# One instruction per tile in place of two, with the activations pinned, in a split GELU-multiply

The kernel runs on one core of one Trainium2 chip (trn2). The metric is the device time of one execution in microseconds (us), lower is better.

## What is computed

```python
x1, x2 = x[..., :1024], x[..., 1024:]          # x: (32, 512, 2048) float32
out = 0.5 * x1 * (1 + erf(x1 / sqrt(2))) * x2  # (32, 512, 1024) float32
```

So 134.2 MB are read, 67.1 MB are written, and each output element needs one GELU and one multiply.

## The kernel before

The 16,384 rows are cut into 16 tiles of 128 partitions x 8 rows. A tile is loaded whole (64 KB per partition, 8.39 MB) and stored whole (32 KB per partition, 4.19 MB). There are two input and two output buffers, so load i+2 can be issued only when tile i has been consumed.

```python
# cut: the pools, the views of x and out, and the store helper; the whole kernel follows below
def load(i):
    x_tile = xpool.tile([P, R, dim], x.dtype, name="x_tile")   # bufs=2
    nc.sync.dma_start(out=x_tile, in_=x_t[i])
    return x_tile

ahead = [load(0), load(1)]
for i in range(n_tiles):
    x_tile = ahead.pop(0)
    o_tile = opool.tile([P, R, half], out.dtype, name="o_tile")  # bufs=2
    last = i == n_tiles - 1
    for lo, hi in ((0, 1), (1, 2), (2, 4), (4, 8)) if last else ((0, 4), (4, 8)):
        rows = slice(lo, hi)
        nc.scalar.activation(out=x_tile[:, rows, :half], in_=x_tile[:, rows, :half], func=GELU)
        nc.vector.tensor_mul(out=o_tile[:, rows, :], in0=x_tile[:, rows, :half], in1=x_tile[:, rows, half:])
        if last and hi % 4 == 0:
            store(nc.sync, i, o_tile, slice(hi - 4, hi))
    if not last:
        store(nc.sync if i == n_tiles - 2 else nc.scalar, i, o_tile, slice(0, R))
    if i + 2 < n_tiles:
        ahead.append(load(i + 2))
```

The engines named here are ACT (ScalarE), DVE (VectorE) and SP (SyncE, which here only issues transfers). Loads are issued from SP, the stores of tiles 0 to 13 from ACT, the last three stores from SP. ACT thus has two jobs in one instruction stream: GELU, and issuing stores that wait for the multiply on DVE.

## Time and profile before

| | before |
|---|---|
| median of the first 3 executions | 471.6 us (471.53 to 471.65) |
| busy ACT / DVE | 115.4 / 140.5 us (25% / 30%) |
| DMA, moved over the span | 201.35 MB, 428 GB/s |
| spacing of the landings in the middle | 29.0 us |

A landing is the moment at which a transfer is complete. The list of DMA issues has, at the right, the size of one transfer in KB where it is known, and the median time from issue to landing:

```profile
out_dram<-o_tile ACTq DMA_DIRECT2D x14, 4096.0 KB, 41.6
...
x_tile<-in_x_dram SPq DMA_DIRECT2D x16, 45.4
```

The waits of the loading queue are given as total us, times, longest:

```profile
SPq L42 <- DMA x_tile<-in_x_dram: 224.8, 14, 21.2
SPq L42 <- DVE o_tile L58: 174.8, 14, 12.8
```

The second line is the time in which the next load waits for the multiply of the tile that holds its buffer: 174.8 / 14 = 12.5 us per load, which is the time from a landing to the end of that tile's compute.

### The profile page before, as it was taken

To read this page: it belongs to the slowest core of one execution; us is meant where nothing else is said; L and a number is where in the kernel's file an instruction comes from. 1 tells how busy PE (TensorE), PEld (TensorE's weight loads), DVE (VectorE), ACT (ScalarE), POOL (GpSimd) and SP (SyncE) were. 2 spreads that over 40 slices of the span, in tenths; PEclk is the share of its full clock that TensorE was granted. 3 is DMA by queue.
4 is the path that set the end of the run, shared out by engine and by line. 5 is a ranking of instruction groups with operands and counts; after the bars stand their busy time and mean duration, and the time that the engine had idled before them with its cause. 6 is when DMAs were issued, how large, how long until landed. Compare 5 with 4: busy or idle time off the path is not lost.

```text
span 470.1 us, 217 instructions
## 1 busy us (share of the span) xinstructions
DVE 140.5 (30%) x34; ACT 115.4 (25%) x35; POOL 0.2 (0%) x4
## 2 busy tenths in 40 slices
DVE  0070703307043070420705106061150601507042
ACT  1051406024060230603206032060410605105060
POOL 0000000000000000000000000000000000000000
DMA  8999999999999999999999999999999999999988
GB/s 357 446 446 357 443 449 446 402 443 449 402 446 441 435 457 404 432 418 485 407 424 421 488 407 413 432 488 407 402 443 482 413 402 443 472 424 402 480 380 346
DMA packets 4754, 201.35 MB, mean 428 GB/s; under 512 B 528, under 2 KB 528, under 8 KB 528
## 3 DMA queue, kind: packets, MB, share of 16 engines
q1 hardware_dynamic: 2736, 142.61, 70.5%
q10 hardware_dynamic: 2016, 58.72, 28.9%
q14 instruction: 2, 0.02, 0.0%
HBM read 134.22 MB, written 67.11 MB: 428 GB/s over the span
## 4 chain that ended last, share of the span: by engine, by line
DMA 77%; DVE 14%; ACT 7%; issue 0%; ACTq 0%; SPq 0%
DMA x_tile<-in_x_dram 77%; DVE o_tile L58 14%; ACT x_tile L55 7%; ACTq L94 0%; SPq L42 0%; ACTq L55 0%
## 5 line engine op out<-in xcount | busy, mean ns | idle before, releaser
L58 DVE TENSOR_TENSOR o_tile<-x_tile 128x4096 f32<-128x4096 f32 (+2 forms) x34 | 140.5, 4171 | 321.2 <-ACT x_tile L55 321.2
L55 ACT ACTIVATE x_tile<-x_tile 128x4096 f32<-128x4096 f32 (+2 forms) x34 | 114.2, 3407 | 341.0 <-DMA x_tile<-in_x_dram 341.0
L55 ACT ACT_TABLE_LOAD x1 | 1.3, 1283 | 0.7 <-PEq L83 0.7
L83 POOL MEMSET const-bfloat16-1.0<- 128x1 bf16 x1 | 0.1, 102 | 0.0
L83 POOL MEMSET const-uint8-127<- 128x1 uint8 x1 | 0.1, 102 | 0.0
L83 POOL MEMSET const-float32-0.0<- 128x1 f32 x1 | 0.1, 99 | 0.2 <-issue 0.2
L83 POOL MEMSET const-float32-1.0<- 128x1 f32 x1 | 0.1, 99 | 0.0
## 6 DMA issues: line engine op xcount, KB each, us to landing
out_dram<-o_tile ACTq DMA_DIRECT2D x14, 4096.0 KB, 41.6
out_dram<-o_tile SPq DMA_DIRECT2D x1, 4096.0 KB, 24.8
out_dram<-o_tile SPq DMA_DIRECT2D x2, 2048.0 KB, 8.0
x_tile<-in_x_dram SPq DMA_DIRECT2D x16, 45.4
```

The lines of the kernel that those rows point to most:

```text
L55: nc.scalar.activation(out=x_tile[:, rows, :half], in_=x_tile[:, rows, :half], func=GELU)
L58: nc.vector.tensor_mul(out=o_tile[:, rows, :], in0=x_tile[:, rows, :half], in1=x_tile[:, rows, half:],)
L83: nc = _bacc.Bacc("TRN2", target_bir_lowering=False, num_devices=1)
```

## The change

Its intent is fewer, larger instructions in tiles 1 to 14: one activation and one multiply of 8192 elements per partition in place of two of each of 4096. The first tile keeps two halves, the last keeps its four steps. As the compiler's ordering pass may float an early-ready activation ahead of a store on ACT, each activation is pinned behind what the program has put before it on that engine; the pin is an edge of order only, without a wait for data.

```diff
-        for lo, hi in ((0, 1), (1, 2), (2, 4), (4, 8)) if last else ((0, 4), (4, 8)):
+        if last:
+            steps = (0, 1), (1, 2), (2, 4), (4, 8)
+        else:
+            steps = ((0, 4), (4, 8)) if i == 0 else ((0, 8),)
+        for lo, hi in steps:
             rows = slice(lo, hi)
-            nc.scalar.activation(
-                out=x_tile[:, rows, :half], in_=x_tile[:, rows, :half], func=GELU
+            tc.keep_in_program_order(
+                nc.scalar.activation(
+                    out=x_tile[:, rows, :half], in_=x_tile[:, rows, :half], func=GELU
+                )
             )
```

## The prediction

> **What bounds the kernel now.** I read first the page for who is busy, then the chain of work that ended last, then the waits of the loading queue, then the timeline of one tile, and last the packet records of the DMA in the trace. The page's head and its DMA rows:
>
> ```profile
> span 470.1 us, 217 instructions
> DVE 140.5 (30%) x34; ACT 115.4 (25%) x35; POOL 0.2 (0%) x4
> DMA  8999999999999999999999999999999999999988
> DMA packets 4754, 201.35 MB, mean 428 GB/s; under 512 B 528, under 2 KB 528, under 8 KB 528
> ```
>
> The reader is to see that both compute engines idle for over two thirds of the span, while the 16 DMA engines are busy at 90% or more in all but the first and last slices. The table of stretches between landings gives DMA share 1.00 and 434 GB/s from 45 to 335 us, stretch after stretch: the kernel is a steady copy, with the arithmetic beside it. The chain of waits seems to tell another story:
>
> ```profile
> by line: DMA x_tile<-in_x_dram 76.7%; DVE o_tile L58 14.0%; ACT x_tile L55 6.8%; issue 0.3%; ACTq L94 0.2%; SPq L42 0.1%; ACTq L55 0.0%
> ...
> 103.35 3.62 ACT x_tile L55
> 106.98 0.02 issue
> 107.00 8.77 DVE o_tile L58 x2
> 115.78 0.02 issue
> 115.79 45.39 DMA x_tile<-in_x_dram
> 161.18 0.02 issue
> ```
>
> It alternates: half a GELU (3.62), two multiplies (8.77), then a load of 45.39 us that their end lets go, two tiles (58 us) per round. Read literally, the compute is 21% of the path. But 45.39 us is from issue to landing, and most of it is not work: 8.39 MB at 434 GB/s would take 19.3 us alone, and the 12.6 MB that a tile moves in all (8.39 in, 4.19 out) take 29.0 us, exactly the spacing of the landings below. The first part of the 45.39 us is waiting in line behind the load before it. The timeline of tile 2 and of the start of tile 3:
>
> ```profile
> 74.42 7.12 ACT L55 ACTIVATE x_tile<-x_tile 128x4096 f32<-128x4096 f32 x2 [22.10 <-DMA x_tile<-in_x_dram]
> 78.07 8.76 DVE L58 TENSOR_TENSOR o_tile<-x_tile 128x4096 f32<-128x4096 f32 x2 [20.46 <-ACT x_tile L55]
> 86.86 29.27 SPq L42 DMA_DIRECT2D x_tile<-in_x_dram  x2
> 86.86 0.36 ACTq L46 DMA_DIRECT2D out_dram<-o_tile  x1
> 103.35 7.12 ACT L55 ACTIVATE x_tile<-x_tile 128x4096 f32<-128x4096 f32 x2 [21.81 <-DMA x_tile<-in_x_dram]
> ```
>
> Tile 2 lands just before 74.42. Its last multiply ends at 86.83, and at 86.86 load 4 and store 2 are both issued. Tile 3 lands only at 103.3, so load 4 stands 16 us in line before the loading queue is free for it. In the packet records load 4's first packet of 65,536 B starts at 102.82, and store 2's first of 32,768 B at 100.39. Those records also show how the two queues share an engine: one load packet (2.42 us), one store packet (1.21 us), in turn, without a hole, 8 of each per tile on each engine: 8 x 3.63 = 29.0 us. Neither queue is ever empty between the first store (first packet 42.39) and the end of store 13 (about 446). From 446 to the last byte, load 15, store 14 and the two halves of store 15 follow each other in one queue, again without a hole.
>
> **What the Trainium skill says.** (1) "DMA: Bandwidth & Descriptors", section "Queues, rings and completion order": each DMA engine goes round-robin between the queues it has work for and switches at packet boundaries. The trace agrees: load and store packets alternate one for one, as 2.42 and 1.21 us. (2) The same page, "Where 436 GB/s comes from": a fabric ceiling of 435.2 GB/s. The trace's 434 GB/s in the steady stretches is that, within half a per cent: no reordering can be worth much here. (3) "ScalarE: Activation LUTs", "What ACT_TABLE_LOAD costs": an activation with immediate scale and bias takes 186 ns + 0.833 ns per element, and two back to back overlap by about 93 ns. The trace agrees: 1895 ns for 2048 elements (formula 1892), 3601 ns for 4096 (3598), two in 7.12 us. (4) "VectorE: DVE Perf Modes", "The TRN2 errata": fp32 tensor_tensor takes (N+151)/0.96 ns. The trace has 2293 ns at N=2048 (formula 2291) and 4420 at 4096 (4424). The forms in the profile:
>
> ```profile
> L58 DVE TENSOR_TENSOR o_tile<-x_tile 128x4096 f32<-128x4096 f32 x31 | 135.8, 4422 | 304.6 <-ACT x_tile L55 304.6
> L55 ACT ACTIVATE x_tile<-x_tile 128x4096 f32<-128x4096 f32 x31 | 110.4, 3608 | 320.6 <-DMA x_tile<-in_x_dram 320.6
> L55 ACT ACTIVATE x_tile<-x_tile 128x2048 f32<-128x2048 f32 x1 | 1.9, 1895 | 0.0
> ```
>
> **The change, part by part.** Tiles 1 to 14 get one activation and one multiply of 8192 elements instead of two each of 4096; tile 0 and tile 15 keep theirs.
>
> Removed: 14 activations and 14 multiplies. From the durations measured at 2048 and 4096, doubling adds 3601 - 1895 = 1706 and 4420 - 2293 = 2127 ns per 2048 elements, so at 8192: 3601 + 2 x 1706 = 7.01 us for ACT, 4420 + 2 x 2127 = 8.67 us for DVE. Busy time falls by 14 x (2 x 3.60 - 7.01) = 2.7 us on ACT and 14 x (2 x 4.42 - 8.67) = 2.4 us on DVE, to about 112.7 and 138.1 us. Both lie beside the DMA and are worth nothing to the end.
>
> Added: the overlap of GELU with the multiply inside a tile is lost. Before, from landing to the last multiply's end: 3.62 + 0.02 + 8.77 = 12.4 us. After: 7.01 + 0.03 + 8.67 = 15.7 us. So in tiles 1 to 14 the store i and the load i+2 are issued 3.3 us later.
>
> Is that later issue on the path? Three margins answer.
> - Load: 102.82 - 86.86 = 16.0 us between issue and first packet, 12.7 after the change. What a transfer really needs: store 0 was issued at 35.24 into an empty queue on busy engines and its first packet started at 42.39, so 7.15 us (an engine finishes packets already taken). 12.7 is more, and the next load keeps its place.
> - Store: 100.39 - 86.86 = 13.5 us, 10.2 after. Also more than 7.15, by 3 us. So the store queue does not run dry either; this is the narrowest margin.
> - Output buffer: tile i+1's multiply needs store i-1 landed. Store 1 is issued at 57.63 and lands 41.5 us later, 99.2; tile 3's multiply starts at 107.0 before and at 110.4 after. The margin grows from 7.8 to 11.
>
> With no queue ever dry, each packet goes at the moment at which it goes now: landings stay 29.0 us apart, and the 45.4 us from issue to landing shrinks to 42.1 by as much as the compute grew. The end is unchanged too: tile 15 lands at 449.8 as before and keeps its four steps; store 14 is issued at 438.1 instead of 434.8, and its first packet is due at 448.40, 10.3 us on, again above 7.15.
>
> The pinning: an activation of tile i+1 now cannot be ordered ahead of store i on ACT. In the trace of before it was not: the store goes at 86.86 and the next activation starts at 103.35, and the same holds in every other tile. If that order had been the other way, the store would have gone after the landing. So the pins keep what is there, presumably because the longer instruction could have tempted the compiler's ordering. Cost 0; it adds order and no wait on data.
>
> Sum: 0 us on the path that sets the end, of 471.6.
>
> **The rivals.**
> - The chain is right as written and each of its rounds grows by 3.3 us. There are seven full rounds of load, GELU and multiply after the first load, and 7 x 3.3 = 23 us: 495 us, 4.9% slower. For it speaks only the chain; against it the DMA row, which has no hole that a late issue could have caused. I give it 1 to 2%.
> - The store queue misses its turn because the needed lead is more than the 7.15 us seen once. Then the engine takes another load packet in its place; it does not idle. Loads come 1.2 us earlier, stores 2.4 us later, the margin heals by itself, and the backlog of stores is moved after load 15, where the engines are busy anyway. Estimate: 0 to +1 us, 471.6 to 472.6.
> - Faster, through 28 fewer instructions and fewer semaphores: only if the compute were on the path. The most it could be is the fixed costs above, and the DMA's floor of 201.3 MB at 434 GB/s is 464 us, with the start (first packet at 1.74) and the final write's receipt on top. I see at most 1 us.
> - An ordering accident: without knowing the compiler's choice, some load or store could sit behind something on SP or ACT. The pins cover ACT; SP's order follows from the data. One displaced tile would cost at most some 16 us of a hidden wait, so little. 1%.
>
> **Range and chances.** The point is the time of before, 471.6 us. Runs of before spread over 0.12 us; another session could be off by a few tenths; the second rival adds up to 1 us. So the range is 470.8 to 472.8 us. A 2% change is 9.4 us, and only the first and the last rival reach it: slower 0.02, faster 0.01, same 0.97.
>
> **What would show each step.** Right: activations of 8192 elements at 7.0 us and multiplies at 8.7 us, 14 of each; load from issue to landing near 42 us, store near 38 us (41.6 less 3.3); landings still 29.0 us apart; the DMA row unchanged; the last tile starting at 449.9. The chain would show compute at a larger share, near 26%, and the DMA at less, at the same span: that is the proof that the chain's shares were not costs. Wrong: landings more than 29.0 us apart, or a digit under 9 in the middle of the DMA row, which means a queue that ran dry on both sides; or issue to landing still at 45.4 us, which would mean that the first rival is true; or an ACT queue in which a store waits for the next landing.

## The result

The changed kernel took 471.9 us (median of 6 executions, 471.81 to 472.19), the kernel before 471.56 us on the same chip (6 executions, 471.34 to 471.69). The ratio is 1.0008, with a 95% interval of 0.9996 to 1.0021: the same.

The page after, in its head and its DMA rows:

```profile
span 469.8 us, 189 instructions
...
DVE 139.5 (30%) x20; ACT 114.1 (24%) x21; POOL 0.2 (0%) x4
...
DMA  8999999999999999999999999999999999999988
```

There are 28 instructions fewer, 1.3 us less of ACT and 1.0 us less of DVE, and the DMA row is the same digit for digit. The groups by form give the new durations (busy us, mean ns, then the idle time before them):

```profile
L64 DVE TENSOR_TENSOR o_tile<-x_tile 128x8192 f32<-128x8192 f32 x14 | 121.7, 8692 | 281.9 <-ACT x_tile L60 281.9
L60 ACT ACTIVATE x_tile<-x_tile 128x8192 f32<-128x8192 f32 x14 | 98.4, 7029 | 301.7 <-DMA x_tile<-in_x_dram 301.7
```

The chain of work that ended last, to be held against the same stretch of before in the prediction (start, duration, what):

```profile
by line: DMA x_tile<-in_x_dram 71.8%; DVE o_tile L64 13.9%; ACT x_tile L60 11.8%; ACTq L100 0.2%; issue 0.2%; SPq L42 0.1%; ACTq L60 0.0%
...
103.87 7.04 ACT x_tile L60
110.91 0.02 issue
110.93 8.70 DVE o_tile L64
119.64 0.02 issue
119.65 42.14 DMA x_tile<-in_x_dram
161.79 0.02 issue
```

The compute of a round grew from 3.62 + 8.77 to 7.04 + 8.70 us, the load from 119.65 took 42.14 us in place of 45.39, and a round of two tiles ends at 161.79 - 103.79 = 58.00 us after the one before, as it did. What was added at one link was taken off the next one. The waits of the loading queue and the DMA issues say the same in other units:

```profile
SPq L42 <- DVE o_tile L64: 217.9, 14, 15.8
SPq L42 <- DMA x_tile<-in_x_dram: 185.2, 14, 21.0
```

```profile
out_dram<-o_tile ACTq DMA_DIRECT2D x14, 4096.0 KB, 36.9
...
x_tile<-in_x_dram SPq DMA_DIRECT2D x16, 42.1
```

The load's issue waits 43.1 us longer for the multiply in all (217.9 - 174.8) and 39.6 us less for a landing (224.8 - 185.2); issue to landing is 3.3 us shorter. The extra wait for compute was time in which a load would otherwise have stood in line.

### The profile page after: what moved, and what is told of

It is laid out like the page before. It is cut to its first block, busy times and chain, and to the rows that moved or that the text cites. A ratio compares the mean times of both kernels' runs of the same rounds, so it can differ in the third digit from the quotient of the medians.

```text
span 469.8 us, 189 instructions
## 1 busy us (share of the span) xinstructions
DVE 139.5 (30%) x20; ACT 114.1 (24%) x21; POOL 0.2 (0%) x4
## 3 DMA queue, kind: packets, MB, share of 16 engines
q10 hardware_dynamic: 2016, 58.72, 28.9%
## 4 chain that ended last, share of the span: by engine, by line
DMA 72%; DVE 14%; ACT 12%; ACTq 0%; issue 0%; SPq 0%
DMA x_tile<-in_x_dram 72%; DVE o_tile L64 14%; ACT x_tile L60 12%; ACTq L100 0%; SPq L42 0%; ACTq L60 0%
## 5 line engine op out<-in xcount | busy, mean ns | idle before, releaser
L64 DVE TENSOR_TENSOR o_tile<-x_tile 128x8192 f32<-128x8192 f32 (+3 forms) x20 | 139.5, 6985 | 321.6 <-ACT x_tile L60 321.6
L60 ACT ACTIVATE x_tile<-x_tile 128x8192 f32<-128x8192 f32 (+3 forms) x20 | 112.8, 5661 | 341.9 <-DMA x_tile<-in_x_dram 341.9
## 6 DMA issues: line engine op xcount, KB each, us to landing
out_dram<-o_tile ACTq DMA_DIRECT2D x14, 4096.0 KB, 36.9
x_tile<-in_x_dram SPq DMA_DIRECT2D x16, 42.1
```

## The experiments

Twelve kernels were run, and all gave the right result. The theory under test is the prediction's: the time is set by the 16 DMA engines, and a later issue costs nothing so long as the queues still hold work (the full-queue theory). Its first rival is the chain taken literally: every microsecond of compute in a round of two tiles costs one microsecond. "E" in a diff stands for the expression that was there. The listing of the compiled instructions gave the order on each engine before each run.

### The pins alone

```diff
 # kernel before
-            nc.scalar.activation(...)
+            tc.keep_in_program_order(nc.scalar.activation(...))
```

> The kernel before with the pins and nothing else. The listing of its instructions shows the same order on every engine as before, so both theories (the DMA's full queues set the time; the chain's compute sets the time) expect the time of before within 0.1%, about 471.6 us. It also serves as a second profile of the order of before: where the first packet of store 0 falls (42.39 us before, 39.94 us after the change) and the median of store from issue to landing (41.6 before, 36.9 after) tell whether that difference is scatter between executions (then it may move here too) or comes from the whole-tile instructions (then 42.4 and 41.6 again).

Measured: 471.58 us, ratio 1.0003 (0.9988 to 1.0018). Store 0's first packet started at 41.98 us and the store's median from issue to landing was 41.7 us, as before. The pins do nothing to the kernel before, whose order already was that of the program. On the second question the run spoke for the whole-tile instructions, but another run (the last tile whole, below) has the change's instructions up to tile 14 and had 42.31 us and 38.5 us, and a third run with the same first tile (twice and four rows, below) had 39.97: so the 39.94 and 36.9 us of the profile after are scatter between executions, by one packet's turn.

### The whole tiles alone, without pins

```diff
 # kernel after
-            tc.keep_in_program_order(nc.scalar.activation(...))
+            nc.scalar.activation(...)
```

> The change without the pins. The compiler then orders two activations ahead of two stores on ACT in three places (the activations of tiles 5, 9 and 13 stand ahead of the stores of tiles 4, 8 and 12), so those stores wait for the next landing, some 13 to 20 us. Full-queue theory: while the store queue is dry the loads run alone and the engines stay busy; what can be lost is a wait of the multiply of tiles 6, 10 and 14 for an output buffer, 0 to 3 us each, so 471.9 to 481 us. Rival, each displaced store costs its delay: 3 x 13 to 20 us on top, 511 to 532 us.

Measured: 477.99 us, ratio 1.0137 (1.0120 to 1.0154). The timeline shows the first displaced store: tile 4's multiply ends at 147.2, and its store goes only after the GELU of tile 5 has its landing, together with the next one ("16.12 ... x2" spans both):

```profile
138.52 8.69 DVE L62 TENSOR_TENSOR o_tile<-x_tile 128x8192 f32<-128x8192 f32 x1 [20.38 <-ACT x_tile L59]
159.08 7.03 ACT L59 ACTIVATE x_tile<-x_tile 128x8192 f32<-128x8192 f32 x1 [20.59 <-DMA x_tile<-in_x_dram]
159.11 16.12 ACTq L46 DMA_DIRECT2D out_dram<-o_tile  x2
```

That store was 11.9 us late, and three such stores cost 6.4 us in all (477.99 - 471.60), not three times 12. The rival of this run (each delay paid in full) falls. The wait for an output buffer that I had named as the loss did not occur three times but once (16.4 us, at the first multiply of the last tile), and that tile's last multiply still ended 11.8 us after the landing, as it does after the change. The loss lies elsewhere: between 161 and 448 us the rate was 426 GB/s, against 434 from 103 to 161. In the packet records the store queue is empty from 154 to 163, and from about 200 us on load packets last up to 3.3 us where 2.42 is the rule (the median; 1.21 for a packet of half the size). Summed over the run, packets take 5.7 us per engine above their rule, against 1.8 after the change, and the engines end further apart (2.4 us from the first to the last, against 0.9). Why those packets are stretched is not settled by this run. What is shown is that the pins belong to the whole-tile form: without them the change costs 1.4%.

### The first tile whole as well

```diff
 # kernel after
-            steps = ((0, 4), (4, 8)) if i == 0 else ((0, 8),)
+            steps = ((0, 8),)
```

> The first tile whole as well. Load 2 and store 0 are then issued at about 38.4 us instead of 35.1, and the engines take their last packets of load 1 at 38.6 and would be done with them at 41.0. Full-queue theory: here both queues are dry for a moment, for the lead of 4.8 to 7.2 us is not there, so part of the 3.3 us is lost: 1 to 3.3 us, 472.9 to 475.2 us. Rival, issue time is hidden everywhere: 471.9 us.

Measured: 471.46 us, ratio 0.9996 (0.9981 to 1.0011). My expectation failed. Load 2 was issued at 38.49 us and its first packet started at 40.99, 2.5 us later, right behind the last packet of load 1. Since store 0 came later too, load 1 was not slowed by it and landed at 42.0 instead of 45.8. An issue into a queue about to run out thus needs at most 2.5 us here, not the 7.15 us that I had read from store 0: in the packet records of the kernel before, that store, issued at 35.24, stood behind two load packets of each engine (on one they start at 36.1 and 38.6). In this run store 0 still took 5.9 us to its first packet (38.49 to 44.34), behind the first packets of load 2; so the 2.5 us is shown for a load. The halving of the first tile in the changed kernel is worth nothing measurable.

### The last tile whole as well

```diff
 # kernel after
-            steps = (0, 1), (1, 2), (2, 4), (4, 8)
+            steps = ((0, 8),)       # and one store of the whole tile
```

> The last tile whole as well, with one store. Load 15 still lands at 449.4; 7.04 + 8.70 us of compute end at 465.2, and the store of 4 MB needs some 12.5 us (the 2 MB one took 8.0 with 5.0 us of packets, so 3.0 + 9.7): end of the span near 478, 8 us longer, time near 480 us. The engines stand idle from about 458 to 466 us. The chain theory expects about the same here: in the last tile nothing hides the compute. A rise of under 3 us would be against both.

Measured: 478.79 us, ratio 1.0150 (1.0135 to 1.0165), 7.2 us more than before. The stretches of the end show it (us, DVE, ACT, POOL busy, clock, DMA share, GB/s):

```profile
core 0: us, DVE busy (x) ACT busy (x) POOL busy (x), PEclk, DMA share, GB/s
449.00:458.00 9.00, 1.57 (x1) 7.03 (x1) 0.00 (x0) 1.00 0.94 408
458.00:466.00 8.00, 7.12 (x1) 0.00 (x0) 0.00 (x0) 1.00 0.05 20
466.00:477.10 11.10, 0.00 (x0) 0.00 (x0) 0.00 (x0) 1.00 0.85 363
```

For 8 us the engines have next to nothing to move while the multiply runs; the span grew by 7.3 us (477.1 against 469.8). Here the same whole-tile instruction that is free in the middle costs 7 us.

### Making the compute shorter and longer

Five runs vary the time from a landing to the end of that tile's multiply. In the first, tiles 1 to 14 go in four steps; in the others the multiply is repeated, with the same result, and pinned in program order.

```diff
 # kernel after: quarters
-            steps = E if i == 0 else ((0, 8),)
+            steps = E if i == 0 else ((0, 2), (2, 4), (4, 6), (6, 8))
 # kernel after: multiply twice (2) and thrice (3)
-            nc.vector.tensor_mul(...)
+            for _ in range(1 if i == 0 or last else 2):
+                tc.keep_in_program_order(nc.vector.tensor_mul(...))
 # kernel after: twice and a part, n = 2 or 4 rows
+            for rows in (rows,) if i == 0 or last else (rows, rows, slice(0, n)):
+                tc.keep_in_program_order(nc.vector.tensor_mul(...))
```

Quarters:

> The opposite direction: tiles 1 to 14 in four steps of 2048 elements each, 56 activations and 56 multiplies in place of 14 and 14. From landing to the last multiply's end 1.89 + 4 x 2.29 = 11.1 us, 4.6 us less than after the change and 1.3 less than before. Full-queue theory: nothing gained or lost, 471.6 to 472.0 us, load from issue to landing about 46.7 us. Chain theory: seven rounds by -4.6 us against the change, about 440 us.

Twice:

> The change with each multiply of tiles 1 to 14 done twice (same result, pinned in program order), to see how much later an issue may come. From landing to the last multiply's end: 7.04 + 2 x 8.70 = 24.4 us instead of 15.7. Full-queue theory: the next landing is still 4.6 us off when the load is issued; if the lead that an issue needs is under that, nothing is lost (472 us); if it is the 4.8 to 7.2 us that store 0 showed, up to 2.6 us are lost per tile in 13 tiles, up to 506 us; I expect about 480. Chain theory: each of the seven rounds of two tiles grows by 8.7 us, 61 us in all, 533 us.

Thrice:

> The same with each multiply done three times: 33.1 us from landing to the last multiply's end, more than the spacing of the landings (29.0), so the load is issued into an empty loading queue. Full-queue theory: two tiles take the compute plus one load of about 29 + 2 us, 64 us for two, 32 us per tile instead of 29: about 13 x 3 = 39 us more, 511 us, with DMA share under 0.95 in the steady stretches. Chain theory: seven rounds by 17.4 us, 122 us, 594 us.

Twice and two rows:

> Each multiply of tiles 1 to 14 done twice, and a third time for two of the eight rows: 7.06 + 17.42 + 2.29 = 26.8 us from landing to the last multiply's end, so the load is issued about 2.2 us before the landing ahead of it is due. Doing the multiply twice (24.4 us) cost nothing, and its loads started 2.0 us after their issue. If the lead that an issue needs is those 2.0 to 2.6 us, this is the edge: 471.9 to 480 us. If the needed lead were 4.8 us or more, as store 0 seemed to say, there would be a hole of some 2.6 us per tile, about 506 us.

Twice and four rows:

> The third time for four of the eight rows: 7.06 + 17.42 + 4.42 = 28.9 us, a lead of 0.1 us. With a needed lead of 2 us both queues are dry for about 2 us per tile: 13 x 2 = 26 us more, 498 us. If only the pins count (the next GELU stands behind the store on ACT, so a tile takes at least 28.9 + 0.45 = 29.4 us of compute), 13 x 0.4 = 5 us more, 477 us.

Measured, with the first column from the timelines (the GELU starts at the landing in all but the last row, where it starts later) and the second the shares of DVE and ACT in the chain that ended last:

| kernel | GELU's start to last multiply's end, us | compute's share of the chain | median, us | ratio to before |
|---|---|---|---|---|
| quarters | 10.8 | 18.4% | 471.55 | 0.9998 (0.9983 to 1.0013) |
| before | 12.4 | 20.8% | 471.56 | |
| after | 15.7 | 25.7% | 471.9 | 1.0008 (0.9996 to 1.0021) |
| multiply twice | 24.5 | 38.7% | 471.94 | 1.0005 (0.9990 to 1.0020) |
| twice and 2 rows | 26.8 | 39.9% | 500.88 | 1.0616 (1.0587 to 1.0646) |
| twice and 4 rows | 28.9 | 41.4% | 512.64 | 1.0868 (1.0830 to 1.0905) |
| multiply thrice | 33.2 | 69.6% | 541.55 | 1.1481 (1.1458 to 1.1504) |

The first four rows are the answer to the main question. Over a range of 13.7 us of compute per tile the time does not move, while the chain's share of compute doubles. The chain taken literally wanted 440 us for quarters and 533 us for the multiply done twice; it is refuted. In the multiply done twice the stretches still have the full rate:

```profile
161.20:219.30 58.10, 34.77 (x4) 14.15 (x3) 0.00 (x0) 1.00 1.00 434
```

Then comes a step of 29 us for 2.3 us more compute per tile, which I had not expected so large: I had said 472 to 480 us at the edge, because the load would still be issued before the landing. The timeline of the run with two rows more shows how near it was (tile 1's multiplies, the store, then the load's issue, then tile 2's GELU at its landing):

```profile
51.71 19.75 DVE L67 TENSOR_TENSOR o_tile<-x_tile 128x8192 f32<-128x8192 f32 x3 [16.67 <-ACT x_tile L60]
71.49 0.37 ACTq L46 DMA_DIRECT2D out_dram<-o_tile  x1
71.52 88.80 SPq L42 DMA_DIRECT2D x_tile<-in_x_dram  x4
72.37 7.03 ACT L60 ACTIVATE x_tile<-x_tile 128x8192 f32<-128x8192 f32 x1 [20.69 <-DMA x_tile<-in_x_dram]
```

The load is issued at 71.52, before the landing at 72.37, but the engines' last packets of the load before ended at 71.1 to 72.0, and the last packet of the store queue had ended at 67.2. The first packet of the new load starts at 72.47. The idle time is 1.2 us per engine; the first load packets then take 3.4 to 4.0 us instead of 2.42. Summed over the run, packets take 22.9 us per engine above their rule, against 2.1 in the multiply done twice: that is 20.8 of the 26.8 us by which the span grew (496.6 - 469.8); the engines' idle time makes up the rest, 5.8 us per engine from the first packet to the last. So most of the loss is not idle time that the DMA row would show but packets that last longer. In the first part of the run they stand at the moments in which both queues change to a new transfer; later they also occur with an issue 6.5 us ahead of the landing, and there I cannot say what stretches them. A busy DVE is not enough to stretch them: it worked 34.8 us of 58 both in this run from 161 to 219 us (405 GB/s) and in the multiply done twice from 161.2 to 219.3 (434 GB/s). My other branch, a hole of 2.6 us per tile and 506 us, is nearer in number to the 500.9, but the engines idled 5.8 us in all and not the 34 us that this branch wanted (13 x 2.6).

With four rows more both of my figures, 498 and 477 us, were too low: it took 512.64. There the packets take 21.8 us per engine above their rule and the engines idle 23.7 us from the first packet to the last, which together account for the 43.7 us of growth (513.5 - 469.8): idle time of about the 26 us expected, and the stretched packets that I had not reckoned with.

For the multiply done thrice I had said 511 us and the chain's rival 594; it took 541.55. The waits (total, times, longest) and the timeline name what I had left out:

```profile
ACT x_tile L60 <- DVE o_tile L66: 293.5, 11, 26.7
```

```profile
213.23 0.37 ACTq L46 DMA_DIRECT2D out_dram<-o_tile  x1
213.26 101.45 SPq L42 DMA_DIRECT2D x_tile<-in_x_dram  x4
213.70 7.03 ACT L60 ACTIVATE x_tile<-x_tile 128x8192 f32<-128x8192 f32 x1 [26.68 <-DVE o_tile L66]
```

The next tile has landed, but its GELU stands behind the store on ACT, and the store waits for the multiply. The GELU before this one started at 180.00, so a tile takes 213.70 - 180.00 = 33.7 us, GELU and multiplies in sequence; 14 x (33.7 - 29.0) = 66 of the 70 us lost.

### The same with the stores on SP

```diff
 # multiply thrice
-            store(nc.sync if i == n_tiles - 2 else nc.scalar, i, o_tile, slice(0, R))
+            store(nc.sync, i, o_tile, slice(0, R))
```

> The multiply three times again, but all stores issued from SP, so that no store stands between two activations on ACT. With the stores on ACT the time was 541.5 us, and the trace shows the next GELU waiting for the multiply (ACT waits for DVE 293 us in all), 33.7 us per tile. If that wait behind the pinned store sets the time there, it is gone here: the GELU of the next tile goes at its landing beside the multiplies, and a tile takes (31 + 7 + 26.2) / 2 = 32 us, or less: 505 to 520 us (the single queue alone costs 4 us, as the run with stores on SP showed). If not the pin but the DMA's late issue sets it, 540 us again.

Measured: 519.24 us, ratio 1.1009 (1.0992 to 1.1026), within what was expected. ACT waits for DVE no more (its waits on the landing are 389 us in all, on DVE none), and 22.3 us are won back. So the stores in ACT's stream, kept ahead of the next activation, do have a price: once the compute of a tile is longer than the 29 us that its bytes take. At 15.7 us it is never asked for.

### Stores on SP alone

The same edit on the changed kernel itself.

> The change with all stores issued from SP, so that loads and stores stand in one queue, whole transfer after whole transfer, and no packets alternate. Full-queue theory: the one queue is never dry (a store and a load are issued 15.7 us after a landing, while the load before still runs), the bytes are the same, so 471.9 us within 1.5, landings 29.0 us apart, store from issue to landing shorter. Rival, the two queues taking turns are themselves needed to fill the engines: over 2% slower, above 481 us, with DMA share under 0.98.

Measured: 475.55 us, ratio 1.0085 (1.0066 to 1.0104). Neither side is right. The rate in the middle is that of after within half a per cent (433 GB/s from 103 to 448 us in both), so two queues in turn are not needed to fill the engines; but the expectation of 471.9 within 1.5 us failed. The span is 3.9 us longer (473.7 - 469.8). By 448 us some 0.5 MB are missing against after (403 instead of 412 GB/s up to 45 us, 432 instead of 434 up to 103 us), which is 1.2 us at 434 GB/s. The rest is lost at the end, where the DMA share is 0.80 instead of 0.90: the engines drift apart from transfer to transfer in this run (load 2's packets are spread over 20.7 us, load 15's over 24.1), so that some have finished while others still move. Why they drift is open.

### Storing earlier in the first tile

```diff
 # kernel after, tile 0
-            steps = ((0, 4), (4, 8)) if i == 0 else ((0, 8),)
+            steps = ((0, 2), (2, 4), (4, 6), (6, 8)) if i == 0 else ((0, 8),)
             ...  # and two stores of four rows each; activations pinned only for i > 0
```

> The change with the first tile in four steps and its store in two halves, to start storing and load 2 earlier: load 2 issued at 33.7 instead of 35.1 us, the first half store at about 29. In every trace so far the last packet of a load before the first store is stretched by 1.0 to 1.5 us per engine. If that stretch is a queue run dry, it goes away: 470.5 us. If it is the price of the first store's arrival, it stays: 471.5 to 472.3 us. I expect the latter.

Measured: 472.62 us, ratio 1.0020 (1.0008 to 1.0033): 1.1 us slower, above what was expected either way, so nothing is to be had there. But the run shows how much the waits can change at nearly the same time. The waits of the multiply, and the chain that ended last:

```profile
DVE o_tile L64 <- DMA out_dram<-o_tile: 280.0, 14, 20.7
```

```profile
by line: DMA out_dram<-o_tile 72.1%; DVE o_tile L64 14.6%; DMA x_tile<-in_x_dram 9.4%; ACT x_tile L59 1.5%; issue 0.2%; DVEq L100 0.2%; DVEq L64 0.1%; SPq L42 0.1%
```

The two first stores have packets of 16 KB, so that in turn with the loads' packets of 64 KB they move half of what stores with packets of 32 KB do. Their packets run from 34.0 to 78.7 us, where store 0 had needed 39.9 to 66.8, and the stores stay behind for the rest of the run: a store now takes 49.1 us from issue to landing, a load 34.8. Fourteen multiplies then wait for an output buffer instead of for a landing, and the chain names the stores with 72% where it named the loads with as much. The middle still moves 434 GB/s.

## Why the prediction was right

- **What bounds the kernel.** Right, and shown by the runs from quarters to multiply twice: equal times with 10.8 to 24.5 us of compute per tile, at 434 GB/s in the steady stretches. What sets the 434 GB/s, the engines themselves or the memory at one of their ends, no run here separates.
- **The cost of each part.** Right: 7029 ns and 8692 ns against 7.01 and 8.67 us, and 15.7 us from landing to the last multiply's end. The busy time saved was half of the prediction's 2.7 and 2.4 us (1.3 on ACT, 1.0 on DVE). The step that failed there is "14 x (2 x 3.60 - 7.01)": two instructions back to back overlap by 0.09 us, which the prediction had cited and not subtracted, so a pair covers 7.12 us on ACT, not 7.20.
- **The margins.** The sign was right, the size off. Load 4 was issued 11.9 us ahead of its first packet (102.55 - 90.66; said: 12.7), store 2 7.8 us (98.42 - 90.66; said: 10.2). The term that was mis-sized is "what a transfer really needs ... 7.15 us": the first tile whole shows that 2.5 us is enough for a load. Had 7.15 been true, the store would have had 0.6 us to spare. The verdict did not hang on that: in the multiply done twice no store packet runs from 67.2 to 73.7 us, the engines go on with loads, and the time is the same. The real edge lies between 24.5 and 26.8 us of compute per tile.
- **"Each packet goes at the moment at which it goes now".** Too strong: the first store moved by one turn between executions, which the time does not feel. "In turn, without a hole" and "neither queue is ever empty" are too strong as well: in the kernel before, no store packet runs on any engine from 67.6 to 71.4 us, although store 1 was issued at 57.63. At each change of transfer the engine takes two packets of the other queue in a row and makes up for it later. What holds is that an engine always had a packet of one queue or the other (from 45 to 448 us it idled under 0.4 us in all).
- **The pinning.** "Cost 0" is right at this size, shown by the pins alone. The prediction saw only half of their use: it said that a displaced store would cost "little" and gave this 1%. Without the pins three stores are displaced and the change costs 1.4%. The pins are a part of the change that works, not a precaution.
- **The rivals.** The chain read literally (495 us) is refuted by all four runs on the plateau. The profile after has no store that came late for its turn; the run without pins, where three stores do, lost about 2 us per displaced store, against the 0 to 1 us in all that the prediction estimated for such a miss.
- **The end.** Load 15 landed at 449.4 (before 449.8), and the four steps of the last tile matter: undoing them cost 7 us.

## What to carry to other kernels

This is shown on one kernel. The chain that ended last tells in which order things waited, not what they cost: a wait from issue to landing that is longer than the transfer's own time contains queueing, and the queueing takes up whatever is added before it, until the engines run dry. So measure the spare time (issue ahead of the moment at which the engines finish what they hold) before judging a longer instruction; what fits into it is free, what exceeds it is paid (here 2.1 us per tile for the 2.3 us beyond 24.5), and at the last tile there is none. Where stores share an instruction stream with compute, keep the order of the program when instructions grow, and remember that the store then holds up the next tile's compute once a tile computes for longer than it transfers.

## What the Trainium skill lacked or had wrong

- "DMA: Bandwidth & Descriptors" (Where 436 GB/s comes from) says that for transfers between HBM and SBUF the HBM side at about 358 GB/s binds. One core alone read and wrote HBM here at 434 GB/s in the steady stretches of before, after and the multiply done twice. The sentence is at odds with the page's own table of single-core measurements, which says that about 358 GB/s is what each core gets with both cores of the HBM domain streaming; no run here has two.
- The same page (Queues, rings and completion order) has the turns between queues, but not what follows for shares: the trace's packets were as long as a partition's row, 65,536 B for loads and 32,768 B for stores, so equal turns gave the loads two thirds of the rate; in the run that halved the first stores' packets and stored earlier, a store took 49.1 us and a load 34.8 us from issue to landing, where it had been 36.9 and 42.1.
- No page that I read has the stretched packets: load packets of 3.4 to 4.9 us instead of 2.42 around late issues, 22.9 us per engine in the run with 26.8 us of compute per tile. In the kernel before the first packets of all, into idle engines, took 2.8 to 3.4 us too. The cause is open.
